# Modulation by matmuls, q and k by tokens, filter norms ahead of the taps, and a priority for the first run, in a hybrid diffusion step on one core

## The chip, the cores and the metric

The kernel runs on one core of a Trainium2 chip. The metric is the device time of one execution in microseconds (us). A core has five engines that run side by side, each with its own list of instructions: TensorE (PE in the profile, its weight loads as PEld), VectorE (DVE), ScalarE (ACT), GpSimd (POOL) and SyncE (SP), which here only issues DMAs. An instruction waits at the head of its engine's list until what it needs is there, and all that stands behind it on that engine waits too.

## The reference

One layer of a hybrid diffusion model, in fp32, on 2048 latent tokens (a grid of 32 by 64) and 256 prompt tokens, width 1024:

```python
shift1, scale1, gate1, shift2, scale2, gate2 = split(silu(cond) @ w_mod + b_mod, 6)
h = rms_norm(x, norm1_g) * (1 + scale1) + shift1
u_pool, u_hy, u_q, u_k, u_v = split(h @ w_in)          # 256, 3*256, 512, 512, 512 columns
y_pool = pool_mixer(u_pool)                            # window means, per-group linear
# Hyena: k = (mlp(z) @ f3_w) * decay, k / (sum over positions of |k| + 1e-6),
# two long convolutions by FFT, gated by a short convolution of u_hy
y_hy = hyena_mixer(u_hy, ...)
q = rms_norm(u_q per head of 64, q_norm_g); k = rms_norm(u_k per head of 64, k_norm_g)
y_na = attend(q, k, v)                                 # latent: 8x16 neighbourhood + 256 cached keys
x = x + gate1 * (concat(y_pool, y_hy, y_na) @ w_out)
h = rms_norm(x, norm2_g) * (1 + scale2) + shift2
x = x + gate2 * (square(relu(h @ w_up)) @ w_down)
```

The latent tokens and the prompt tokens have different conditioning vectors, so the modulation has two sets of six vectors of 1024. Outputs: both token sets, and the prompt's normalised k and its v.

## The kernel before

**Products.** Every wide product is made of three: each operand is split into a high and a low half (`split`, ACT or POOL makes the high half, DVE the low one as the difference), and `mm3` multiplies high by high, low by high and high by low. An accumulator in PSUM is 128 x 512. Weights come in tiles of 512 KB (`wtile`): a DMA, a high half (1024 columns a partition), a low half `wl` on DVE.

**Three streams.** The program is written as three generators that are woven by declared costs: `dense`, `latent_mixers` and `prompt_mixers`, the last two with priorities behind it (1000 and 2500). A scheduler then puts the instructions of each engine in an order by priority and readiness; that order is fixed when the program is built.

**dense.** `modulation_first` multiplies silu of both conditions by the first 2048 columns of w_mod: 16 slabs `wm` of 128 x 1024, four column strips of the PE array, 32 products (L239), then four transposes; this gives shift1 and scale1. The u projection follows in five runs of 512, 512, 512, 256 (the prompt) and 512 tokens, in the order UORD; a run normalises its 8 blocks of x (`normed`) and multiplies eight weight tiles `w_u`, each 24 products of 512 columns. The q, k and v projection (`proj_qkv`, runs in the order QORD) takes ten jobs a run. For q and k, channels are the rows of the result: a tile of 128 channels (two heads) by all tokens of the run, 24 products; ACT copies it and squares it, POOL and DVE split the square, two products with `headsum` (L265) add up the squares of a head's 64 channels and spread the sum over its 64 rows, `rstd` makes the root in six wide steps on ACT and DVE (L144 and L145 are the DVE ones), and DVE applies root and gain. For v, tokens are the rows: 128 tokens by 256 channels, 24 products of 256 columns. Then come the prompt's output projection and MLP, and those of the latent bands.

**The other four modulation vectors** (`modulation_rest`) are made in steps that `dense` interleaves with the jobs (MODU steps behind each u tile of a run, MODQ behind every second step of q, k and v): for each of 8 chunks of 512 columns and each of 8 slabs of 128 rows, DVE adds the slab times one condition to an accumulator (L338), ACT scales it by the other (L339) and POOL adds that (L340); at the end of a chunk eight products with ones (L346, 2 columns) add up the 128 partitions.

**Filters** (`filters`, in latent_mixers, beside the u projection). A small MLP with sines makes h2 (64 features, two directions, 2304 positions). `filter_taps` multiplies it by f3 (16 tiles of 128 positions for each of two filters, L405), DVE multiplies by the decay (L411), ACT takes the absolute value and POOL adds it up (L414). When all taps of a filter are there, `filter_rinv` adds over positions by products with ones, and POOL divides each tile (L419). Then comes the first half of the FFT (`time_to_freq`; the low half of its input is `ksl`). The rest of the Hyena mixer (`hyena`: the first halves for z, 16 groups of `spectrum` a filter, the inverse) runs beside q, k and v, the prompt's mixers too, and the latent attention after it.

**The order in time**, from the first and the last product of each: the first u product stands at 66 us; u runs to about 430 us; q, k and v to 1049; the Hyena mixer to about 1200; the latent attention from 1224 to 2000, with output projections and MLPs beside it; MLPs of the bands fill the rest.

The lines that the prediction's steps touch follow.

Of the kernel before, what the change touches and what calls it, by code (L numbers as in the profile page):

```python
# [10 lines left out]
F32 = mybir.dt.float32  # L11
# [8 lines left out]
P = 128  # L20
# [7 lines left out]
DH = 64  # L28
# [27 lines left out]
def tile_hybrid_step(ctx: ExitStack, tc: tile.TileContext, a: dict):  # L56
# [33 lines left out]
    headsum = ctile([P, P], "headsum", F32R)  # L90
    for e in range(2):
        for f in range(2):
            nc.gpsimd.memset(headsum[64 * e:64 * e + 64, 64 * f:64 * f + 64].bitcast(F32), float(e == f))

# [40 lines left out]
    def rstd(pool, ss, n, shape):  # L135

        r = pool.tile(shape, F32, tag="rsr", name="r", bufs=1)
        v = xp.tile(shape, F32, tag="tmp", name="v")
        t = xp.tile(shape, F32, tag="tmp", name="t")
# [80 lines left out]

    def modulation_first(lp):
# [18 lines left out]
        pmt = acc_tile()  # L240
        mrow = xp.tile([P, 512], F32, tag="raw", name="mrow", bufs=3)
        nc.vector.tensor_copy(mrow, pm)
        for q in range(4):
            nc.tensor.transpose(pmt[:, q * P:(q + 1) * P], mrow[:, q * P:(q + 1) * P], ident)
        pmv = pmt.rearrange("p (q j r) -> p j q r", q=4, j=4)

        def halves(t):
            return t.rearrange("p (j q) -> p j q", j=2)

# [6 lines left out]
    JOBS = ((1, 0), (1, 1), (1, 2), (1, 3), (2, 0), (0, 0), (0, 1), (0, 2), (0, 3), (2, 1))  # L256

    def proj_qkv(qp, hT, T0, n):
# [3 lines left out]
        def finish(comp, j, raw, sq):  # L262
            pss = aux_tile()[:, :n]
            for i in range(2):
                nc.tensor.matmul(pss, headsum, sq[i], start=(i == 0), stop=(i == 1))  # L265
            r = rstd(qp, pss, DH, [P, n])
            nc.vector.scalar_tensor_tensor(out=raw, in0=raw, scalar=(qg8, pvs("kg"))[comp], in1=r, op0=ALU.mult, op1=ALU.mult)
            nc.sync.dma_start(out=(qT, kT)[comp][j][:, T0:T0 + n], in_=raw)
            if comp == 1 and T0 == NL:
                nc.sync.dma_start(out=a["new_kT"][j * P:(j + 1) * P, :], in_=raw)  # L270

        def rows(dst, r0, cs):
            return dst[r0:r0 + 2 * P, cs].rearrange("(e p) c -> p e c", p=P)

        for comp, part in JOBS:
            if comp == 2:
                W = [wtile("w_v", 2 * part + kk, 4, (None, nc.gpsimd)[kk]) for kk in range(2)]
                cs = slice(part * 256, (part + 1) * 256)
                for t in range(0, n, 2 * P):
                    pp = acc_tile()  # L280
                    for e in range(2):
                        ts = slice(t + e * P, t + (e + 1) * P)
                        for k in range(KD):
                            mm3(pp[:, e * 256:(e + 1) * 256], hT[k][0][:, ts], hT[k][1][:, ts], W[k // 4][0][:, k % 4, :], W[k // 4][1][:, k % 4, :], k == 0, k == KD - 1, skip_group_check=True)
                        yield 2600
                        while todo:
                            finish(*todo.pop(0))
                    v = qp.tile([P, 2, 256], F32, tag="q", name="v")
                    nc.scalar.activation(v.rearrange("p e c -> p (e c)"), pp, AF.Copy)
                    if T0 < NL:  # L290
                        nc.sync.dma_start(out=rows(vd, T0 + t, cs), in_=v)
                    else:
                        nc.sync.dma_start(out=rows(vpd, 0, cs), in_=v)
                        nc.sync.dma_start(out=rows(a["new_v"], 0, cs), in_=v)
                continue
# [4 lines left out]
            while todo:  # L300
                finish(*todo.pop(0))
# [1118 lines left out]
```

## Time and profile before

| | |
|---|---|
| median of 3 executions | 3247.18 us (3244.32 to 3251.28) |
| the profiled execution | 3239.31 us, of which the span of its instructions is 3237.4 us |
| mean granted clock of PE | 0.959 |
| PE busy | 3008.9 us (93% of the span) |
| DVE busy | 2104.9 us (65%) |
| ACT busy | 1507.1 us (47%) |
| POOL busy | 1179.4 us (36%) |

These are averages over stages that differ. The page's slices show POOL and DVE at 30 to 90% in the first 15 of 40 slices (some 1200 us) and at 20 to 60% later, and PE's clock at 0.8 or 0.9 of its full rate in most of the first 15 and above 0.9 in all later ones. A wait in the rows below is put down to the instruction that ended last before it, which is not always the one that would have been late alone.

### The profile page before, as it was taken

To read this page: it belongs to the slowest core of one execution; us is meant where nothing else is said; L and a number is where in the kernel's file an instruction comes from. 1 tells how busy PE (TensorE), PEld (TensorE's weight loads), DVE (VectorE), ACT (ScalarE), POOL (GpSimd) and SP (SyncE) were. 2 spreads that over 40 slices of the span, in tenths; PEclk is the share of its full clock that TensorE was granted. 3 is DMA by queue.
4 is the path that set the end of the run, shared out by engine and by line. 5 is a ranking of instruction groups with operands and counts; after the bars stand their busy time and mean duration, and the time that the engine had idled before them with its cause. 6 is when DMAs were issued, how large, how long until landed. Compare 5 with 4: busy or idle time off the path is not lost.

```text
span 3237.4 us, 44877 instructions
## 1 busy us (share of the span) xinstructions
PE 3008.9 (93%) x15997; PEld 2483.3 (77%) x15997; DVE 2104.9 (65%) x3090; ACT 1507.1 (47%) x2803; POOL 1179.4 (36%) x996
## 2 busy tenths in 40 slices
PE   4989888878898899999999999899999999999999
PEld 1777677766777898986887777688878888788887
DVE  8797967997857977787666555544463444644443
ACT  3556455554656656666555554322342223432222
POOL 3777745566424523445333332311131111311111
PEclk8999888888998999999999999999999999999999
DMA  6657476556855596553334324322324223232322
GB/s 220 190 161 250 140 231 218 188 189 195 274 173 190 163 313 196 180 186 107 123 114 126 111 94 154 115 96 98 124 85 150 98 93 122 91 118 97 98 98 85
DMA packets 252862, 489.99 MB, mean 151 GB/s; under 512 B 23508, under 2 KB 124569, under 8 KB 252316
## 3 DMA queue, kind: packets, MB, share of 16 engines
q1 hardware_dynamic: 245437, 464.83, 44.1%
q0 software_dynamic: 7200, 22.28, 2.4%
q8 instruction: 127, 2.08, 0.3%
q14 instruction: 98, 0.79, 0.1%
HBM read 417.67 MB, written 70.13 MB: 151 GB/s over the span
## 4 chain that ended last, share of the span: by engine, by line
PE 68%; DVE 15%; DMA 6%; issue 4%; POOL 4%; ACT 3%; SPq 1%; DVEq 0%; ACTq 0%; POOLq 0%
PE pm L131 19%; PE pm L132 19%; PE pm L133 19%; PE po L867 3%; PE ppt L846 2%; DVE wl L120 2%; PE ps L832 1%; PE ps L833 1%; DMA dc<-in_decay 1%; POOL kk L419 1%; DVE macc L338 1%; DMA wm<-in_w_mod 1%; DVE hl L171 1%; PE pf L131 1%; POOL ssq L155 1%
## 5 line engine op out<-in xcount | busy, mean ns | idle before, releaser
L131 PE MATMUL pm<-hh,wh 128*128 128x512 f32 (+1 forms) x2240 | 850.0, 382 | 37.8 <-ACT hh L117 17.6
L120 DVE TENSOR_TENSOR wl<-wraw,wh 128x1024 fp32r<-128x1024 f32 x460 | 608.0, 1323 | 424.7 <-ACT wh L117 403.6
L132 PE MATMUL pm<-hl,wh 128*128 128x512 f32 (+1 forms) x2240 | 847.6, 379 | 16.7 <-DVE hl L171 12.4
L133 PE MATMUL pm<-hh,wl 128*128 128x512 f32 (+1 forms) x2240 | 845.1, 378 | 6.7 <-DVE wl L120 6.7
L117 ACT ACTIVATE wh<-wraw 128x1024 fp32r<-128x1024 f32 x430 | 454.5, 1058 | 765.7 <-PE pm L132 673.5
L120 POOL TENSOR_TENSOR al<-r,ah 128x512 fp32r<-128x512 f32 (+1 forms) x160 | 200.8, 1256 | 975.2 <-ACT ah L117 975.0
L131 PEld LDWEIGHTS pm<-hh,wh 128*128 128x128 f32 x2240 | 435.0, 195 | 116.8 <-ACT hh L117 19.1
L132 PEld LDWEIGHTS pm<-hl,wh 128*128 128x128 f32 x2240 | 434.6, 194 | 95.8 <-DVE hl L171 14.8
L133 PEld LDWEIGHTS pm<-hh,wl 128*128 128x128 f32 x2240 | 433.8, 194 | 81.9 <-DVE wl L120 8.0
L133 PE MATMUL pm<-ah,wl 128*128 128x512 f32 (+1 forms) x1280 | 475.8, 372 | 0.1
L131 PE MATMUL pm<-ah,wh 128*128 128x512 f32 (+1 forms) x1280 | 471.9, 372 | 4.0 <-ACT ah L117 2.5
L132 PE MATMUL pm<-al,wh 128*128 128x512 f32 (+1 forms) x1280 | 474.1, 371 | 1.2 <-POOL al L120 1.2
L1094 DVE SCALAR_TENSOR_TENSOR x<-pm,gate,x 128x512 f32<-128x512 f32 (+1 forms) x320 | 221.1, 695 | 273.3 <-PE pm L133 272.5
L131 PEld LDWEIGHTS pm<-ah,wh 128*128 128x128 f32 x1280 | 240.4, 188 | 47.0 <-ACT ah L117 2.7
L132 PEld LDWEIGHTS pm<-al,wh 128*128 128x128 f32 x1280 | 241.4, 189 | 43.7 <-POOL al L120 1.4
L133 PEld LDWEIGHTS pm<-ah,wl 128*128 128x128 f32 x1280 | 241.4, 189 | 41.8 <-issue 0.8
L838 POOL TENSOR_SCALAR sS<-sS,rl 128x736 f32<-128x736 f32 (+5 forms) x128 | 117.7, 920 | 201.1 <-DVE rl L837 127.2
L969 POOL TENSOR_TENSOR Tt<-bias,mask 128x360 f32<-128x360 f32 (+5 forms) x96 | 102.4, 1067 | 180.1 <-DVE m L981 147.5
L117 ACT ACTIVATE ah<-r 128x512 fp32r<-128x512 f32 (+1 forms) x160 | 93.8, 588 | 151.4 <-DVE r L1077 150.9
L155 POOL TENSOR_TENSOR ssq<-ssq,sqr 128x512 f32<-128x512 f32 (+1 forms) x70 | 97.7, 1396 | 135.5 <-ACT sqr L154 135.5
L986 ACT ACTIVATE sS<-sS,m 128x480 f32<-128x480 f32 (+5 forms) x128 | 77.2, 603 | 112.0 <-DVE m L985 107.7
L1077 DVE TENSOR_TENSOR r<-r 128x512 f32<-128x512 f32 (+1 forms) x160 | 118.1, 739 | 1.5 <-ACT r L1076 1.3
(317 smaller groups left out, 5044.7 us busy)
## 6 DMA issues: line engine op xcount, KB each, us to landing
wraw<-in_w_up SPq DMA_DIRECT2D x160, 512.0 KB
wraw<-in_w_down SPq DMA_DIRECT2D x160, 512.0 KB
wraw<-in_w_u SPq DMA_DIRECT2D x40, 512.0 KB
dftw<-in_S POOLq DMA_DIRECT2D x40, 512.0 KB, 6.4
wraw<-in_w_qk SPq DMA_DIRECT2D x40, 512.0 KB
wraw<-in_w_out SPq DMA_DIRECT2D x40, 512.0 KB
x<-in_xT_sample SPq DMA_DIRECT2D x64, 256.0 KB
wm<-in_w_mod SPq DMA_DIRECT2D x64, 256.0 KB
```

What stands on the lines that cost most here:

```text
L117: nc.scalar.activation(hi, raw, AF.Copy)
L120: lo_eng.tensor_tensor(out=lo, in0=raw, in1=hi.bitcast(F32), op=ALU.subtract)
L131: nc.tensor.matmul(out, lh, rh, start=start, stop=False, **kw)
L132: nc.tensor.matmul(out, lh, rl, start=False, stop=False, **kw)
L133: nc.tensor.matmul(out, ll, rh, start=False, stop=stop, **kw)
L155: nc.gpsimd.tensor_tensor(out=acc, in0=acc, in1=sq, op=ALU.add)
L838: nc.gpsimd.tensor_scalar(out=sc_[:, :tot], in0=sc_[:, :tot], scalar1=r, scalar2=1.0, op0=ALU.mult, op1=ALU.mult)
L867: nc.tensor.matmul(po[64 * e:64 * e + 64, ocol:ocol + P], vap(e, n), pt[:n, col * P:(col + 1) * P], start=(q == 0), stop=(q == len(chunks) ...
L969: nc.gpsimd.tensor_tensor(out=t_, in0=bias[e][:, bro:bro + nr, bco:bco + ncol], in1=mask[rc * 3 + cc_], op=ALU.add)
L986: nc.scalar.activation(sS[:, :n], sS[:, :n], AF.Exp, bias=m4[:, 2:3], accum_out=m4[:, 3:4])
L1077: nc.vector.tensor_tensor(out=r, in0=r, in1=r, op=ALU.mult)
L1094: nc.vector.scalar_tensor_tensor(out=xs[j], in0=po, scalar=gate2[:, j, c:c + 1], in1=xs[j], op0=ALU.mult, op1=ALU.add)
```

## The change

Four parts, in one diff.

1. *First run at the highest priority.* Loads of x, `modulation_first`, the statistics and the normalisations of the first run are written under a priority of 5000.
2. *Filter norms first.* Before any tap, 32 products of 512 fp32 columns compute every tap once with channels as rows; DVE multiplies by the transposed decay `dt`, ACT takes the absolute value and adds it up along the positions in the same instruction. The reciprocals go into `f3n`, so `normed_taps` yields taps that are divided already. POOL's accumulations and divisions, and `filter_rinv`, are gone.
3. *Modulation by matmuls.* `modulation_rest` takes two halves of 2048 columns; for each of 8 slabs of rows four products with `sc` (32 columns of weights, one column strip of PE each) go into one bank, and ACT or DVE adds the bank to a sum in SBUF; four transposes at the end of a half. Its 16 steps stand behind every second tile (MODU, MODQ).
4. *q and k by tokens.* They are computed as v is: 128 tokens are the rows, 256 channels (four heads) the columns, six jobs a run. The sum of squares of a head is a sum along a row on DVE, the root is made on 16 columns at most, DVE multiplies by it, four transposes turn the 256 tokens back to channels as rows, and ACT applies the gain on the way out. `headsum` is gone.

```diff
-    def rstd(pool, ss, n, shape):
+    def rstd(pool, ss, n, shape, size=None):
...
+    def modulation_rows(pmt, rows):
+        mrow = xp.tile([P, 512], F32, tag="raw", name="mrow", bufs=3)
+        nc.vector.tensor_copy(mrow, rows)
+        for q in range(4):
+            nc.tensor.transpose(pmt[:, q * P:(q + 1) * P], mrow[:, q * P:(q + 1) * P], ident)
...
-    JOBS = ((1, 0), (1, 1), (1, 2), (1, 3), (2, 0), (0, 0), (0, 1), (0, 2), (0, 3), (2, 1))
+    JOBS = ((1, 0), (1, 1), (2, 0), (0, 0), (0, 1), (2, 1))
...
+        def finish(comp, part, t, raw, r, out):
+            heads = raw.rearrange("p (e h d) -> p (e h) d", e=2, h=4)
+            nc.vector.tensor_tensor(out=heads, in0=heads, in1=r[:, t // 32:t // 32 + 8, None].to_broadcast([P, 8, DH]), op=ALU.mult)
+            tr = aux_tile()
+            for c in range(2):
+                for e in range(2):
+                    nc.tensor.transpose(tr[:, (2 * c + e) * P:(2 * c + e + 1) * P], raw[:, e * 256 + c * P:e * 256 + (c + 1) * P], ident)
+            nc.scalar.activation(out[:, :, t:t + 256], tr.rearrange("p (c t) -> p c t", c=2), AF.Copy, scale=(qg8, pvs("kg"))[comp])
...
+            for t in range(0, n, 2 * P):
+                pp = acc_tile()
+                for e in range(2):
+                    ts = slice(t + e * P, t + (e + 1) * P)
+                    for k in range(KD):
+                        mm3(pp[:, e * 256:(e + 1) * 256], hT[k][0][:, ts], hT[k][1][:, ts], W[k // 4][0][:, k % 4, :], W[k // 4][1][:, k % 4, :], k == 0, k == KD - 1, skip_group_check=True)
+                    if e == 0 and todo:
+                        finish(*todo.pop(0))
+                    yield 2600
+                v = qp.tile([P, 512], F32, tag="q", name="v", bufs=3)
+                nc.scalar.activation(v, pp, AF.Copy)
+                if comp < 2:
+                    sq = xp.tile([P, 512], F32, tag="tmp", name="sq")
+                    nc.scalar.activation(sq, v, AF.Square)
+                    nc.vector.tensor_reduce(out=ss[:, t // 32:t // 32 + 8], in_=sq.rearrange("p (h d) -> p h d", d=DH), axis=AX.X, op=ALU.add)
...
+            if comp < 2:
+                r = rstd(qp, ss, DH, [P, n // 32], "small")
...
+        for half in range(2):
+            acc = lp.tile([P, 512], F32, tag="macc", name="macc", bufs=1)
             for k in range(KD):
+                for g in range(4):
+                    wm.append(lp.tile([P, 512], F32, tag="wm2", name="wm2", bufs=4))
...
+                for g in range(4):
+                    nc.tensor.matmul(pb[32 * g:32 * g + 32, :], sc[:, k, :], wm[g], start=True, stop=True, skip_group_check=True)
                 if k == 0:
+                    nc.scalar.activation(acc, pb, AF.Copy)
                 else:
+                    nc.vector.tensor_tensor(out=acc, in0=pb, in1=acc, op=ALU.add)
...
+            with scope("norms") as fp:
+                sums = fp.tile([P, 8, 4], F32, tag="sums", name="sums", bufs=1)
...
+                                pf = psum()
+                                nc.tensor.matmul(pf, f3[r, o * 256 + c * P:o * 256 + (c + 1) * P], h2[r, b * 512:(b + 1) * 512], start=True, stop=True)
+                                junk = fp.tile([P, 512], F32, tag="junk", name="junk")
+                                nc.vector.tensor_tensor(out=junk, in0=pf, in1=dt, op=ALU.mult)
+                                nc.scalar.activation(junk, junk, AF.Abs, accum_out=sums[:, j, b:b + 1])
+                        yield 1700
...
+                nc.vector.tensor_tensor(out=f3n, in0=pf, in1=f3, op=ALU.mult)
...
-                    ri = filter_rinv(fp, psum, acc)
                     if o:
                         yield from wait_for("u", "ln")
...
-                        filter_finish(fp, o, kf, 0, ri, i == 0)
-                        filter_finish(fp, o, kb, 1, ri, i == 0)
...
-    MODU, MODQ = (0, 1, 1, 1, 2), (0, 2, 2, 1, 1)
+    MODU, MODQ = (0, 1, 1, 1, 0), (0, 1, 1, 1, 1)
...
+                with tc.high_priority(FIRST):
+                    xs = norm1_load(lp, 0, 512)
+                    modulation_first(m1)
+                    r = norm1_stats(lp, xs)
...
-                    for _ in range(MODU[i]):
+                    for _ in range(MODU[i] if step % 2 else 0):
                         next(mods, None)
```

The line numbers shift: mm3 is L131 to L133 before and L126 to L128 after.

**SP at the start.** SP issues the loads. `x` are blocks of the input, `wm` of 1024 columns the slabs of `modulation_first`, `wm` of 512 columns those of `modulation_rest`, `wraw` weight tiles, `z` the position features of the filter network, `pv` the small vectors (conditions, biases, gains). Before:

```order
L443 DMA z<-in_zT 33x2x2304
L385 DMA f_744<-in_f_w 64x512 x2
L73 DMA pv<-in_pv 128x112
L75 DMA kv<-in_kv 128x34
L315 DMA x<-in_xT_sample 128x512 x8
L236 DMA wm<-in_w_mod 128x1024 x8
L315 DMA x<-in_xT_sample 128x512
L127 DMA wraw<-in_w_u 128x1024 x3
L333 DMA wm_1131<-in_w_mod 128x512
L333 DMA wm_1247<-in_w_mod 128x512
L236 DMA wm<-in_w_mod 128x1024 x8
```

After, behind 8 blocks of x, 8 slabs, the small filter weights and z:

```order
L73 DMA pv<-in_pv 128x112
L75 DMA kv<-in_kv 128x34
L322 DMA x<-in_xT_sample 128x512
L122 DMA wraw<-in_w_u 128x1024 x3
L343 DMA wm_1175<-in_w_mod 128x512
L343 DMA wm_1177<-in_w_mod 128x512
L343 DMA wm_1179<-in_w_mod 128x512
L343 DMA wm_1181<-in_w_mod 128x512
L1192 DMA rsd<-r 1x512
L244 DMA wm<-in_w_mod 128x1024 x2
L122 DMA wraw<-in_w_u 128x1024
L244 DMA wm<-in_w_mod 128x1024 x6
```

x and the first 8 slabs moved ahead of z and pv; the last slabs got one more weight tile, two more slabs of the rest and the store of r in front of them.

**PE in the u projection.** `pm` is the accumulator of a u tile, `hh` and `hl` the halves of the input, `n` the auxiliary bank, `macc` the sum of `modulation_rest`. Before:

```order
L133 MATMUL pm<-hh,wl 128x512 x2
L131 MATMUL pm<-hh,wh 128x512
L346 MATMUL n<-ones,macc 128x2 x4
L131 MATMUL pf<-ksh,dftw 128x256
L346 MATMUL n<-ones,macc 128x2
L132 MATMUL pf<-ksl,dftw 128x256
L133 MATMUL pf<-ksh,dftw 128x256
```

After, at the first group of modulation products (the last row is a product of the norms):

```order
L126 MATMUL pm<-hh,wh 128x512
L346 MATMUL n<-wm_1527,sc 32x512
L346 MATMUL n<-wm_1529,sc 32x512
L346 MATMUL n<-wm_1531,sc 32x512
L346 MATMUL n<-wm_1533,sc 32x512
L127 MATMUL pm<-hl,wh 128x512
L128 MATMUL pm<-hh,wl 128x512
L126 MATMUL pm<-hh,wh 128x512
L127 MATMUL pm<-hl,wh 128x512
L511 MATMUL pf<-h_394,f_739 128x512
```

Eight sums over macc at the end of a chunk gave way to four products on four slabs, once a step, and each norm product stands alone among u products.

**PE at the end of q, k and v.** `pf` is a bank of the spectrum, whose operands are `skh`/`skl` (the filter), `s2h`/`s2l` (the signal) and `ysh`/`ysl` (their product). Before, the last sum over heads stands here, and the next dense product (the prompt's output projection) two rows later:

```order
L265 MATMUL n<-sqh,headsum 128x512
L131 MATMUL pf<-s2h,S2d 128x256
L132 MATMUL pf<-s2l,S2d 128x256
L133 MATMUL pf<-s2h,S2d 128x256
L131 MATMUL pf<-s2h,S2d 128x256
L132 MATMUL pf<-s2l,S2d 128x256
L133 MATMUL pf<-s2h,S2d 128x256
L265 MATMUL n<-sql,headsum 128x512
L131 MATMUL pf<-ysh,S2d 128x256
L131 MATMUL pm<-hh,wh 128x256
L132 MATMUL pm<-hl,wh 128x256
L133 MATMUL pm<-hh,wl 128x256
```

After, the first rows are the last products of v, and `pb` from `sS` belongs to the prompt's attention:

```order
L127 MATMUL pm<-hl,wh 128x256
L128 MATMUL pm<-hh,wl 128x256
L126 MATMUL pf<-ysh,S2d 128x256
L127 MATMUL pf<-ysl,S2d 128x256
L128 MATMUL pf<-ysh,S2d 128x256
L126 MATMUL pf<-ysh,S2d 128x256
L127 MATMUL pf<-ysl,S2d 128x256
L128 MATMUL pf<-ysh,S2d 128x256
L953 MATMUL pb<-ident,sS 128x128 x4
L126 MATMUL pf<-skh,S2d 128x256
L127 MATMUL pf<-skl,S2d 128x256
L128 MATMUL pf<-skh,S2d 128x256
```

From there to the next dense product stand 289 products, 223 of them of the spectrum, the others of the prompt's attention; the longest such run in the order of before has 56.

## Rows read from the trace of the kernel before

**Rows 1.** Stretches: us, busy (instructions) of PE, PEld, DVE, ACT, POOL; clock, DMA, GB/s.

```profile
66.00:430.00 364.00, 311.69 (x1411) 251.00 (x1412) 306.46 (x364) 184.56 (x298) 260.73 (x180) 0.89 0.58 182
430.00:1230.00 800.00, 690.64 (x4255) 610.45 (x4254) 641.38 (x834) 462.84 (x856) 387.28 (x354) 0.91 0.67 216
1230.00:2000.00 770.00, 761.85 (x4950) 622.32 (x4950) 530.21 (x1189) 447.81 (x1123) 296.93 (x287) 0.99 0.42 130
2000.00:3237.40 1237.40, 1214.58 (x5278) 993.51 (x5278) 575.05 (x616) 387.70 (x493) 215.13 (x154) 0.99 0.33 109
```

**Rows 2.** Waits of PE, 66 to 430 us: total us, times, longest.

```profile
PE pf L132 <- DVE ksl L120: 10.8, 7, 2.6
...
PE n L543 <- DVE S2m L350: 0.4, 1, 0.4
```

**Rows 3.** Waits of PE, 430 to 1230 us.

```profile
PE n L265 <- DVE sql L120: 12.3, 12, 1.9
PE pf L131 <- ACT F L590: 11.6, 7, 3.8
...
PE pm L131 <- DVE x L1057: 0.6, 1, 0.6
```

**Rows 4.** Groups of DVE by shape, whole run: busy us, mean ns | idle before.

```profile
L338 DVE SCALAR_TENSOR_TENSOR macc<-wm,sc,macc 128x512 f32<-128x512 f32 x56 | 54.6, 976 | 16.9 <-DMA wm<-in_w_mod 16.8
L984 DVE TENSOR_REDUCE m<-ps 128x1 f32<-128x256 f32 x128 | 53.5, 418 | 60.8 <-PE ps L833 60.3
...
L144 DVE SCALAR_TENSOR_TENSOR t<-t,v 128x512 f32<-128x512 f32 x40 | 36.4, 910 | 31.9 <-ACT t L143 31.9
...
L145 DVE SCALAR_TENSOR_TENSOR r<-t,r 128x512 f32<-128x512 f32 x40 | 33.7, 842 | 0.8
L120 DVE TENSOR_TENSOR sql<-sq,sqh 128x512 fp32r<-128x512 f32 x32 | 30.3, 946 | 15.7 <-POOL sqh L119 15.7
...
L411 DVE TENSOR_TENSOR kk<-pf,dc 128x512 f32<-128x512 f32 x32 | 21.6, 682 | 12.2 <-DMA dc<-in_decay 11.5 <-PE pf L405 0.6
```

**Rows 5.** The low half of a weight tile, 66 to 430 us, then 2000 us on.

```profile
L120 DVE TENSOR_TENSOR wl<-wraw,wh 128x1024 fp32r<-128x1024 f32 x40 | 66.5, 1662 | 8.9 <-ACT wh L117 8.9
...
L120 DVE TENSOR_TENSOR wl<-wraw,wh 128x1024 fp32r<-128x1024 f32 x217 | 270.0, 1245 | 341.2 <-ACT wh L117 335.7
```

**Rows 6.** Groups of POOL, 66 to 430 us.

```profile
L419 POOL TENSOR_TENSOR kk<-kk,rinv 128x512 f32<-128x512 f32 x32 | 52.8, 1686 | 1.1 <-DVE rinv L395 1.1
L414 POOL TENSOR_TENSOR acc<-acc,ab 128x512 f32<-128x512 f32 x32 | 49.4, 1552 | 25.5 <-ACT ab L413 25.2
L340 POOL TENSOR_TENSOR macc<-macc,wm 128x512 f32<-128x512 f32 x30 | 45.8, 1528 | 43.3 <-ACT wm L339 43.0
```

**Rows 7.** Groups of PE, whole run; then PE's timeline: start, us, records.

```profile
L346 PE MATMUL n<-ones,macc 128*128 128x2 f32 x128 | 17.4, 254 | 3.9 <-DVE macc L338 3.6 <-POOL macc L340 0.3
...
L159 PE MATMUL n<-ssq,ones 128*128 128x512 f32 x8 | 4.4, 631 | 0.3 <-POOL ssq L155 0.3
...
51.19 1.92 PE L239 MATMUL pm<-wm,sc 128*32 128x512 f32 x16
...
374.47 1.09 PE L543 MATMUL n<-ident,cy 128*128 128x128 f32 x4 [5.45 <-DVE halo L532]
```

**Rows 8.** Stretches that PE fills: with products of 256, then of 512 columns.

```profile
1150.00:1200.00 50.00, 50.00 (x429) 50.00 (x429) 37.15 (x49) 32.65 (x51) 11.24 (x17) 1.00 0.92 312
2150.00:2200.00 50.00, 50.00 (x221) 41.12 (x220) 21.54 (x24) 15.83 (x20) 6.44 (x5) 1.00 0.29 95
```

**Rows 9.** PE's timeline at the first u products [idle before and its releaser].

```profile
66.40 1.65 PE L131 MATMUL pm<-hh,wh 128*128 128x512 f32 x3 [5.24 <-ACT hh L117]
...
79.21 0.80 PE L132 MATMUL pm<-hl,wh 128*128 128x512 f32 x1 [7.53 <-DVE hl L171]
```

**Rows 10.** PE's timeline where the spectrum is nearly alone.

```profile
1040.92 0.58 PE L131 MATMUL pf<-ysh,S2d 128*128 128x256 f32 x1 [3.82 <-ACT F L590]
...
1050.98 0.58 PE L131 MATMUL pf<-ysh,S2d 128*128 128x256 f32 x1 [1.54 <-ACT ysh L117]
```

More of the change, by code (lines that the diff above doesn't have):

```diff
@@ L89, in tile_hybrid_step @@
     nc.vector.memset(epsc, EPS)
[L90 to L93, printed above, removed]
     uT = [dtile([P, T], f"uT{i}") for i in range(8)]
@@ L239, in modulation_first @@
                     nc.tensor.matmul(pm[r:r + 32, :], sc[:, k, :], wm[:, j * 512:(j + 1) * 512], start=(k == 0), stop=(k == KD - 1), skip_group_check=True)
[L240 to L248, printed above, removed]
+        pmv, halves = modulation_rows(acc_tile(), pm)
         for c in range(2):
@@ new lines, in finish @@
+        def finish(comp, part, t, raw, r, out):
[6 more added lines that the diff above has]
+            nc.scalar.activation(out[:, :, t:t + 256], tr.rearrange("p (c t) -> p c t", c=2), AF.Copy, scale=(qg8, pvs("kg"))[comp])
+            if t + 256 < n:
+                return
+            for c in range(2):
+                j = 2 * part + c
+                nc.sync.dma_start(out=(qT, kT)[comp][j][:, T0:T0 + n], in_=out[:, c])
+                if comp == 1 and T0 == NL:
+                    nc.sync.dma_start(out=a["new_kT"][j * P:(j + 1) * P, :], in_=out[:, c])
@@ L341, in modulation_rest @@
                 yield 600
-            pb = aux_tile()
-            for c in range(2):
-                for j in range(4):
-                    q = 2 * (c * 4 + j)
-                    nc.tensor.matmul(pb[:, q:q + 2], acc[c][:, j * P:(j + 1) * P], ones[:, 0:2], start=(q == 0), stop=True, skip_group_check=True)
-            pbv = pb[:, 0:16].rearrange("p (c j e) -> p c j e", c=2, e=2)
-            dst, nm = ((gate1, "bm_g1"), (S2m, "bm_s2"), (G2, "bm_c2"), (gate2, "bm_g2"))[kind]
-            for c in range(2):
-                nc.vector.tensor_tensor(out=dst[:, half * 4:half * 4 + 4, c], in0=pbv[:, c, :, 0], in1=pvs(nm, half * 4, 4), op=ALU.add)
+            pmv, halves = modulation_rows(aux_tile(), acc)
@@ L351, in modulation_rest @@
+            for j, (dst, nm) in enumerate((((gate1, "bm_g1"), (S2m, "bm_s2")), ((G2, "bm_c2"), (gate2, "bm_g2")))[half]):
+                for c in range(2):
+                    nc.vector.tensor_tensor(out=halves(dst[:, :, c]), in0=pmv[:, 2 * j:2 * j + 2, :, c], in1=halves(pvs(nm, 0, 8)), op=ALU.add)
             yield 1000
```

145 lines of the change are left out of this document (75 added, 70 removed).

## The prediction

> **What bounds the kernel now.** I read the table by stretches first [rows 1]. From 1230 us to the end TensorE is busy 761.9 of 770.0 and 1214.6 of 1237.4 us at a granted clock of 0.99: nothing that a vector engine saves can shorten that, and the change touches no line there. What lies before is different. Until the first product of the u projection at 66.4 us [rows 9] the kernel waits for the modulation vector. From 66 to 1230 us TensorE is busy 311.7 of 364.0 and 690.6 of 800.0 us, at 0.89 and 0.91 of the clock. That is 52.3 + 109.4 = 161.7 us of idle time; and as the clock has two levels (1.2 and 2.4 GHz), 0.89 and 0.91 mean that it stood at the lower one for 22% and 18% of these stretches, after such gaps, which costs up to 40 + 72 = 112 us more. So of 1164 us TensorE needs some 890 at full rate (77%). DVE is busy 306.5 and 641.4 us there, 948 of 1164 (81%), as much as TensorE's own need. The waits say which of the two sets the pace: in the first stretch the rows of TensorE's waits that name DVE run from ksl to S2m, 9 rows that sum to 45.0 of 52.3 us [rows 2]; in the second 11 rows, from sql to x, 40.2 of 109.4 us [rows 3]. DVE therefore ends 85 of 162 us, about half; the rest ends on ACT for the most part. This is a stretch that two engines share, not one with a single bound.
>
> **The start.** x, the first 8 slabs of w_mod and the statistics move ahead of the filter network on SP, TensorE, ACT and DVE; z and pv go behind them. It is less than it looks: in both orders all 16 slabs, three weight tiles and x must land before the modulation is whole, and the order of after puts one more weight tile, two more slabs of the rest and the store of r ahead of the last six. The same bytes at the same rate give no earlier last slab. What can go is what stood after it: the first product came at 66.40 us, and the second weight product only at 79.21 after a wait on hl, which stood on DVE behind filter work [rows 9]; in the new order hl follows the normalisations almost directly. I take 7 us off, with 0 and 14 (most of 79.21 − 66.40) as ends.
>
> **What DVE loses between 66 and 1230 us.** Removed: 56 modulation steps, 54.6 us, and 8 first steps at the same price, 7.8 [rows 4]. For q and k, 32 wide rounds of four instructions (two of the root, the low half of the square, the gain): 32 × (910 + 842 + 946 + 842 ns) = 113 us, where the gain is priced as the second root step; 8 rounds of half the width, 14 us. Together 190 us. Added: 36 sums over head columns; the nearest row is a reduction of 256 columns at 418 ns, so 418 to 836 for 512; 627 gives 23 us. 36 products with the root, at 842: 30. 32 products of the norms and 14 additions from PSUM, at 682: 31 [rows 4]. 40 root steps on 16 columns, below 418 each, 10 us at 250. Together 94. Net 96 us less; with the reduction at either end 88 to 104.
>
> DVE also gets faster where POOL is quiet. The low half of a weight tile takes 1662 ns between 66 and 430 us, with POOL busy 260.7 of 364.0 us (72%), and 1245 after 2000 us [rows 5], with POOL busy 215.1 of 1237.4 us (17%) [rows 1]. POOL loses the accumulations of the modulation and of the norms and the scaling of the taps, 45.8 + 49.4 + 52.8 = 148 of its 260.7 us there [rows 6], which leaves 31%. On the line between the two prices that gives about 1350 ns; 40 tiles × 0.3 = 12 us, and I add half as much for other instructions of DVE that read what lies in SBUF: 18 us, from 12 to 25. DVE's relief is 114 us.
>
> **What TensorE gains in work.** q and k: 768 products of 512 columns and 192 of 256 become 1728 of 256. The stretch that is dense in 512s holds 221 in 50 us (226 ns), the one of 256s 429 in 50 us (117 ns) [rows 8]: 202.2 − 173.6 − 22.5 = +6 us. Norms: 32 products of 512 fp32 columns; the nearest is the column sum of the statistics, 4.4 us for 4 whose last parts overlap other work (8 records, two for an fp32 product) [rows 7]: 0.97 each is taken, 31 us, and 35 at most. Modulation: 16 groups of four products in four column strips, 1.92 us for two such groups (16 records) [rows 7]: 15, against 17.4 us of the old column sums that go [rows 7]. 36 groups of four transposes, 1.09 us by the row, of which the last part overlaps the next product, so from 0.6: 22 to 39, and 25 is taken, nearer to the low end since in a dense order it always overlaps. Against them 80 head sums, 64 × 226 + 16 × 117 ns = 16 us. Small rest (mrow, rib, less the sums of the taps): −1. That is +43 us, with 40 and 61 as ends. Taps and decays of the second filter move behind u; their count stays the same. ACT's saved instructions are not counted: they are slack where DVE or TensorE is late.
>
> **Waits.** Three new ones stand in TensorE's own order. The sums of q and k no longer wait for squares: those waits, 12.3 us on sql, go [rows 3]. The transposes that come instead stand 48 to 126 u, q, k or v products behind the last product of their tile (36 groups), over 5.6 us at 117 ns; the chain before them (copy, square, sum, six root steps, product) has no row of its own on ACT; at DVE's 842 for a wide step and 250 for a small one it costs 2 × 842 + 627 + 6 × 250 + 842 ns = 4.7 us, so it is hidden while neither engine is far behind; with the cover gone it is up to 36 × 4.7 = 167 us, which would be a run slower than before by itself. Modulation products wait for slabs, four at a time with four buffers; one group per two u steps (24 products × 226 ns × 2 = 10.8 us) hides a transfer. The norms go through two PSUM banks, one product per some ten others: a DVE product of 682 ns is hidden by 2 us of others.
>
> **The sum.** If DVE kept its share of 81%, 114 us of relief would shorten the stretch by 140 us; TensorE would then need 890 + 43 = 933 of 1024 us, 91%, against 77% now, with chains from engine to engine still in between. If DVE's relief bought nothing, the stretch would lengthen by TensorE's 43. As DVE ends about half of TensorE's waits [rows 2, 3], I take half of 140, 70 us: 1094 us, with TensorE needing 85% and DVE at 76%. With the start: 3239.3 − 70 − 7 = 3162 for a profiled execution (span 3237.4 and 1.9 around it), and the median of three is 7.9 above that one: **3170 us**; its own range is 3130 to 3215.
>
> **A rule that speaks against it.** In this trace narrow products cost little more: 2 × 117 against 226 ns [rows 8], so halving the columns is worth 6 us. The Trainium skill, TensorE: Matmul & The Clock Gate, section Back-to-back issue gap, says that weight load and product together set the spacing, about 81 ns at 128 columns and 131 at 512. By an estimate on the line between these figures 256 columns would take 98 ns, and the 768 wide products would cost 49 us more instead of 6, which makes 3213. The trace disagrees at 512 columns (226 ns).
>
> **Rivals.**
> - *TensorE sets the pace (slower).* Its waits are the tails of chains that stay as long as before; DVE's relief only lengthens DVE's idle time, and 43 us of fp32 norms, modulation and transposes are added between 66 and 1230 us: 3239.3 − 7 + 43 + 7.9 = 3283. For it: TensorE is already busy 86% there [rows 1], and over half of the second stretch's waits do not name DVE [rows 3]. Against: sql goes, and 45 of 52 us in the first stretch are DVE's [rows 2]. It decides once waits and low clock together shrink by less than 36 us.
> - *A hole behind q, k, v.* In the new order the prompt's convolution and attention slide behind the first spectrum; 289 products then stand in a row without a dense one, 223 of them of the second spectrum. At 117 ns they take 34 us; but the spectrum, 36 products a group, starts a group 10.1 us after the last one where little else is dense [rows 10], and 6.2 groups take 63 us. That is 29 us more: 3199. Against: DVE, busy 641.4 of 800 us [rows 1], has less to do.
> - *The priority does nothing at the start*, since pv and the last slabs come as late: 3177.
> - *Narrow products wait for their weights.* A load takes 41.12 / 221 = 186 ns [rows 8]; if it were not hidden, the pairs would cost 768 × (372 − 226) = 112 us; half of that in place of the 6 gives 3170 + 56 − 6 = 3220. Against: in the row of 256s loads and products are both busy all 50 us at 117 ns. The rule above is the same rival at its own price.
> - *Full relief*: DVE keeps its share, 3239.3 − 7 − 140 + 7.9 = 3100.
> - *No change*: relief and extra work cancel, 3247.
>
> **How the numbers follow.** Forecast 0.48, hole 0.14, priority idle 0.08, full relief 0.08, narrow products 0.04, no change 0.05, slower 0.13. Faster by over 0.2% (about what a measurement of this kernel tells from no change) is 0.82, within it 0.05, slower 0.13. The range leaves out most of the slower case and the lowest part of full relief: 3105 to 3262.
>
> **What would show it.** First u product and second weight product: before 66 and 79 us, expected 3 to 10 earlier. TensorE idle from there to the start of attention: under 110 us against 161.7, clock above 0.93. DVE some 95 to 115 us less busy there, POOL at least 56 × 1.53 + 49.4 + 52.8 = 188 us less over the run [rows 6], wl below 1450 ns in the u projection. Narrow products 117 to 120 ns apart. It is wrong if TensorE's idle time stays, if waits on norms or modulation slabs appear over 15 us each, or if behind q, k, v TensorE is busy under 60% for over 60 us.

## The result and the profile after

The changed kernel takes **3208.5 us** (median of 4, 3195.9 to 3209.6) against 3249.2 for the kernel before: a ratio of 0.987, 95% interval 0.984 to 0.990. The prediction said 3170, from 3105 to 3262. The direction holds; of 77 us forecast, 41 came. One execution with one convolution buffer (5076 us) and one with the priority alone (5469 us) ran at a much lower clock and are left out of the times below; with the first, that kernel's median is the 3188.5 us which the expectations name, without it 3186.8.

(One correction to what stands ahead: the numbers 1000 and 2500 of the two latter streams lift their instructions ahead of `dense`; they are not behind it.)

The profiled execution after took 3209.6 us, span 3207.8. These are its stretches, cut where stages end: first u product, end of u, end of q, k and v, last product of the prompt's attention, first and last product of the latent attention (columns as in [rows 1]).

```profile
0.00:58.40 58.40, 24.48 (x102) 5.64 (x102) 30.42 (x65) 20.02 (x27) 15.48 (x17) 0.97 0.79 273
58.40:390.00 331.60, 314.36 (x1445) 220.82 (x1445) 243.74 (x372) 173.97 (x305) 109.63 (x86) 0.96 0.67 214
390.00:940.00 550.00, 507.65 (x3725) 473.77 (x3726) 372.70 (x522) 268.76 (x531) 218.99 (x207) 0.96 0.69 225
940.00:1030.00 90.00, 67.17 (x350) 53.75 (x349) 68.92 (x110) 51.92 (x113) 39.54 (x31) 0.80 0.41 128
1030.00:1133.00 103.00, 84.55 (x640) 81.98 (x640) 67.76 (x92) 54.26 (x93) 34.90 (x43) 0.91 0.82 258
1133.00:1872.00 739.00, 719.71 (x4948) 599.80 (x4948) 525.62 (x1199) 443.88 (x1121) 297.21 (x287) 0.99 0.45 138
1872.00:3207.80 1335.80, 1313.19 (x5697) 1070.47 (x5696) 613.39 (x661) 417.04 (x537) 228.71 (x163) 0.99 0.33 107
```

The same three stages of the kernel before (start; q, k and v; from there to the latent attention):

```profile
0.00:66.40 66.40, 30.18 (x110) 6.01 (x111) 52.19 (x91) 24.54 (x35) 19.30 (x23) 0.85 0.69 246
...
430.00:1049.00 619.00, 527.72 (x3011) 453.83 (x3009) 491.36 (x626) 354.71 (x676) 320.30 (x287) 0.91 0.65 208
1049.00:1224.60 175.60, 158.56 (x1217) 153.10 (x1217) 144.84 (x197) 104.95 (x174) 64.69 (x66) 0.93 0.73 238
```

The latent attention starts at 1133 instead of 1224.6 us, 92 earlier, yet the end comes only 30 earlier (span 3207.8 against 3237.4). The lead is partly an illusion of order: before, 924 products of 256 columns of the output projections and MLPs stood ahead of the attention, after 534, so 390 × 117 ns = 46 us of the same work was merely put off. The new feature is the fourth row: 90 us behind q, k and v in which TensorE is busy 67 us at a clock of 0.80. There is the hole of the second rival, and its waits (us in total, times, longest) are links of the spectrum's chain:

```profile
PE pf L126 <- DVE Yt L650: 7.8, 5, 2.2
PE pf L126 <- ACT sg L661: 6.0, 7, 1.6
PE pf L126 <- ACT ysh L112: 3.8, 4, 1.6
```

To compare whole executions I use a **ledger** of TensorE. Idle time is the span less PE's busy time on the page. The time of each PE record (up to the start of the next) times the granted clock in it, summed, is the work at full clock; what is left is lost to the low clock. Profiled executions, us:

| kernel | span | idle | lost to low clock | work at full clock |
|---|---|---|---|---|
| before | 3237.4 | 228.5 | 93.7 | 2915.2 |
| changed | 3207.8 | 176.7 | 64.3 | 2966.8 |
| changed, one convolution buffer | 3188.4 | 159.2 | 63.3 | 2966.0 |
| changed, no norms | 3142.5 | 152.7 | 54.4 | 2935.4 |
| changed, no norms, one convolution buffer | 3162.2 | 170.3 | 57.7 | 2934.2 |
| modulation and q, k, one convolution buffer | 3172.4 | 175.6 | 56.6 | 2940.2 |
| modulation by matmuls alone | 3227.0 | 214.4 | 79.8 | 2932.8 |
| q and k by tokens alone | 3220.3 | 209.7 | 88.8 | 2921.8 |
| priority alone | 3280.2 | 261.4 | 97.4 | 2921.4 |

So the change took 52 us of idle time and 29 us of low clock away and added 52 us of work: 30 us in these executions. The medians differ by 41; the profiled execution of before is 8 to 10 us faster than the medians. The last column is not a count of products alone: between before and priority alone, which have the same products, it differs by 6 us, so a few us in it are order.

The prices after, first of PE, then of DVE (busy us, mean ns | idle before), the answers to [rows 7], [rows 4] and [rows 5]; the last row is of 58 to 390 us:

```profile
L511 PE MATMUL pf<-h,f 64*128 64x512 f32 x64 | 36.8, 659 | 3.9 <-DVE junk L514 3.1 <-DVE fx L484 0.8
...
L346 PE MATMUL n<-wm,sc 128*32 128x512 f32 x128 | 24.3, 605 | 0.5 <-DMA wm<-in_w_mod 0.5
L271 PE MATMUL n<-ident,v 128*128 128x128 f32 x144 | 22.1, 277 | 1.8 <-DVE v L267 1.6
```

```profile
L267 DVE TENSOR_TENSOR v<-v,r 128x512 f32<-128x512 f32 x36 | 26.6, 774 | 0.6
L303 DVE TENSOR_REDUCE ss<-sq 128x8 f32<-128x512 f32 x36 | 24.4, 679 | 24.1 <-ACT sq L302 24.0
L514 DVE TENSOR_TENSOR junk<-pf,dt 128x512 f32<-128x512 f32 x32 | 21.8, 684 | 21.0 <-PE pf L511 9.9 <-DMA dt<-in_decayT 7.9 <-ACT macc L348 2.4
```

```profile
L115 DVE TENSOR_TENSOR wl<-wraw,wh 128x1024 fp32r<-128x1024 f32 x40 | 53.1, 1329 | 25.1 <-ACT wh L112 23.5 <-PE n L594 1.3 <-PE pm L128 0.2
```

### The profile page after: what moved, and what is told of

The parts are those of the page before. It is cut to its first block, busy times and chain, and to the rows that moved or that the text cites. A ratio compares the mean times of both kernels' runs of the same rounds, so it can differ in the third digit from the quotient of the medians.

```text
span 3207.8 us, 46233 instructions
## 1 busy us (share of the span) xinstructions
PE 3031.1 (94%) x16901; PEld 2506.2 (78%) x16901; DVE 1922.6 (60%) x3017; ACT 1429.8 (45%) x2722; POOL 944.5 (29%) x832
## 4 chain that ended last, share of the span: by engine, by line
PE 65%; DVE 2%; DMA 1%; ACT 1%; issue 1%; POOL 1%; SPq 0%; ACTq 0%; POOLq 0%; DVEq 0%
PE pm L126 18%; PE pm L128 18%; PE pm L127 18%; PE po L918 3%; PE ppt L897 3%; PE ps L883 1%; PE ps L884 1%; DMA yraw<-yT 1%; PE pf L126 0%; PE pf L127 0%; PE pf L128 0%; POOL ssq L150 0%; PE pbo L957 0%; DVE xn L169 0%; DVE wl L115 0%
## 5 line engine op out<-in xcount | busy, mean ns | idle before, releaser
L126 PE MATMUL pm<-hh,wh 128*128 128x512 f32 (+1 forms) x1920 | 721.0, 378 | 29.0 <-ACT hh L112 14.7
L127 PE MATMUL pm<-hl,wh 128*128 128x512 f32 (+1 forms) x1920 | 718.8, 375 | 1.6 <-POOL hl L115 1.6
L128 PE MATMUL pm<-hh,wl 128*128 128x512 f32 (+1 forms) x1920 | 719.5, 375 | 0.0
L126 PE MATMUL pm<-ah,wh 128*128 128x512 f32 (+1 forms) x1280 | 473.6, 372 | 4.9 <-ACT r L1127 4.0
L128 PE MATMUL pm<-ah,wl 128*128 128x512 f32 (+1 forms) x1280 | 476.4, 373 | 0.0
L126 PEld LDWEIGHTS pm<-hh,wh 128*128 128x128 f32 x1920 | 366.6, 191 | 104.2 <-ACT hh L112 17.2
L128 PEld LDWEIGHTS pm<-hh,wl 128*128 128x128 f32 x1920 | 366.2, 191 | 76.8 <-issue 15.5
L127 PEld LDWEIGHTS pm<-hl,wh 128*128 128x128 f32 x1920 | 366.8, 191 | 75.0 <-issue 9.4
L126 PEld LDWEIGHTS pm<-ah,wh 128*128 128x128 f32 x1280 | 241.1, 189 | 48.2 <-ACT r L1127 4.2
L128 PEld LDWEIGHTS pm<-ah,wl 128*128 128x128 f32 x1280 | 241.7, 189 | 42.6 <-issue 1.5
L126 PE MATMUL pm<-wh,hh 128*128 128x256 f32 x864 | 248.5, 292 | 4.4 <-ACT hh L112 3.9
L127 PE MATMUL pm<-wl,hh 128*128 128x256 f32 x864 | 248.1, 290 | 4.5 <-DVE wl L115 4.4
L128 PE MATMUL pm<-wh,hl 128*128 128x256 f32 x864 | 248.9, 292 | 3.1 <-POOL hl L115 3.1
L126 PEld LDWEIGHTS pm<-wh,hh 128*128 128x128 f32 x864 | 166.8, 194 | 11.1 <-ACT hh L112 5.8
L127 PEld LDWEIGHTS pm<-wl,hh 128*128 128x128 f32 x864 | 167.5, 194 | 7.6 <-DVE wl L115 5.5
```

The costliest lines, as they stand in the source:

```text
L126: nc.tensor.matmul(out, lh, rh, start=start, stop=False, **kw)
L127: nc.tensor.matmul(out, lh, rl, start=False, stop=False, **kw)
L128: nc.tensor.matmul(out, ll, rh, start=False, stop=stop, **kw)
```

## The experiments

All on the chip, each against runs of the kernel before on the same chip (3246.7 to 3250.3). Four things were in question: whether the hole behind q, k and v holds the missing gain, what each part is worth with the others, what it is worth alone, and whether the priority does anything. The runs were taken on three chips, on which the kernel before took 3250.3, 3246.7 and 3249.0 us, so a difference between runs of two chips is good to some 4 us.

### The hole: one buffer less

In the built program the prompt Hyena's pool starts at byte 159,200 of a partition, since the pools of the rest of the modulation and of q, k and v grew by 2048 and 4352 bytes; the pool of the latent mixer's first spectrum ends at 161,120. They overlap by 1920 bytes, and the prompt's mixers stand still after their filters (last product at 490 us) until that spectrum is over: its last product starts at 767 us, their next load is issued at 770. Before, the pools lay 4 KB apart, and that load was issued at 649 us, over 100 us ahead of the spectrum's last product. Two ways of taking 2 KB away:

```diff
-        u = hy.tile([P, L], F32, tag="cu", name="cu", bufs=2)
+        u = hy.tile([P, L], F32, tag="cu", name="cu", bufs=1)
...
-        y = hy.tile([P, L], F32, tag="cy", name="cy", bufs=2)
+        y = hy.tile([P, L], F32, tag="cy", name="cy", bufs=1)
```

> The changed kernel, with one buffer instead of two for the two tiles of the prompt's short convolution (cu, cy). That makes the prompt Hyena's pool 2 KB smaller, so it no longer lies on memory that the latent mixer's first spectrum uses (161,248 against an end of 161,120; in the changed kernel 159,200). Theory 1, the hole is a memory overlap and costs time: the prompt's attention ends before q, k and v do, the stretch of 90 us behind q, k and v in which TensorE was busy 67 us at a clock of 0.80 goes, and with it 23 us of idle time and some 14 us of low clock: 3172 us, from 3160 to 3185. Theory 2, the latent chain sets the end and the dense work only moves: idle time turns up elsewhere and the time stays within 6 us of 3208.5.

Measured: **3186.8 us** (3182.5 to 3190.2), ratio 0.981 (0.979 to 0.982).

```diff
-                v = qp.tile([P, 512], F32, tag="q", name="v", bufs=3)
+                v = qp.tile([P, 512], F32, tag="q", name="v", bufs=2)
```

> The changed kernel with two instead of three buffers for the copies of q, k and v: the same 2 KB, taken from another pool. Theory 1 (memory overlap): the same gain as with one convolution buffer, within 8 us, though waits of ACT on a free copy may cost some of it: 3165 to 3190 us. If the gain of the other run came from the convolution's buffers themselves, this run stays at 3208. Theory 2 (the end is set by the latent chain): both stay at 3208.

Measured: **3198.5 us**, 0.984 (0.983 to 0.986). In both the hole is gone: with one convolution buffer that load is issued at 519 us, and the prompt's attention ends at 817 and 821 us. The same 70 us in the changed kernel, then with one convolution buffer:

```profile
960.00:1030.00 70.00, 52.27 (x253) 41.05 (x253) 50.98 (x82) 38.11 (x83) 30.37 (x24) 0.77 0.32 98
```

```profile
960.00:1030.00 70.00, 57.17 (x397) 54.60 (x396) 61.76 (x85) 41.59 (x76) 35.64 (x29) 0.85 0.64 204
```

144 more instructions went through TensorE, the longest stretch without a dense product ahead of the latent attention fell from 92.6 to 32.3 us, but the gain is 22 and 10 us instead of 37: both times lie between the ranges of the two theories. The stretch is no full one now either: a chain from spectrum to inverse remains in it. And filling has a price elsewhere: with one convolution buffer, idle time and low clock behind q, k and v fall from 63 to 37 us, but during q, k and v, where the prompt's attention now stands, they rise from 59 to 69.

### Without the norms, with and without the overlap

Part 2 undone: taps, absolute values on ACT, sums and divisions on POOL as before.

```diff
-            with scope("norms") as fp:
...
-                        kf, kb = normed_taps(fp, psum, f3n, o, lambda r, e: h2[r, i + e:NL:16], lambda d: a["decay"][d, :, i:i + 2, :])
...
+                    ri = filter_rinv(fp, psum, acc)
...
+                        filter_finish(fp, o, kf, 0, ri, i == 0)
+                        filter_finish(fp, o, kb, 1, ri, i == 0)
```

With one convolution buffer:

> The changed kernel with one convolution buffer (no overlap), and with the filters as before: taps first, POOL adds up and divides. Compared with 3188.5 us. By the prediction's sum the norms cost TensorE 31 us and DVE 22 us and relieve POOL of 102 us, which makes DVE some 12 us faster: without them the kernel is 15 to 37 us faster, 3150 to 3173. The rival: POOL's chain sets the pace of the u projection (adding up, dividing, then the FFT), and without the norms the kernel is slower, 3200 to 3225.

Measured: **3163.5 us**, 0.974 (0.973 to 0.976): 23 us faster than with the norms. And with two buffers, so with the overlap:

> The changed kernel with the filters as before, and with the overlap of pools (159,200 against 161,120). Without the overlap it took 3163.5 us. In the order of this kernel the last product of the prompt's attention stands ahead of the last one of q and k, so dense work does not run out: if the overlap costs only through that hole, 3163 within 6; if it costs by itself, 3183 (the 20 us of the changed kernel) or more.

Measured: **3144.6 us**, 0.968 (0.966 to 0.970), the fastest of all, 64 us ahead of the changed kernel (2%). Neither expectation holds: here the overlap does not cost 22 us, it gives 19. (It does hold the prompt back: the load that was issued at 770 us in the changed kernel is issued at 703 us with it and at 601 without.) From the end of q, k and v to the latent attention, first with the overlap, then without:

```profile
962.00:1098.30 136.30, 121.86 (x958) 118.93 (x958) 108.42 (x146) 81.28 (x136) 49.93 (x55) 0.94 0.79 261
```

```profile
972.00:1119.00 147.00, 127.91 (x985) 124.45 (x984) 115.20 (x155) 86.30 (x147) 52.47 (x58) 0.91 0.76 248
```

With the overlap the prompt's attention ends at 957 us, 5 us before q, k and v do (962), so dense work never runs out; without it, at 858. Idle time over the run is 152.7 against 170.3 us. A late prompt is thus no harm in itself: it puts its small products beside more of q, k and v. It harms where it ends after them, as in the changed kernel (1030 against 940 us). This reading fits both pairs; it was not tried by moving the prompt alone.

### Without the priority, and the priority alone

```diff
-                with tc.high_priority(FIRST):
-                    xs = norm1_load(lp, 0, 512)
-                    modulation_first(m1)
-                    r = norm1_stats(lp, xs)
+                xs = norm1_load(lp, 0, 512)
+                modulation_first(m1)
+                r = norm1_stats(lp, xs)
...
```

> The changed kernel without the priority of the first run. By the prediction's step on the start the first u product comes some 7 us later than with it (58.4 us) and the time is 3216 us (3209 to 3223). The rival that the priority does nothing: 3208. A third reading, that early filter work matters more than an early first run, would make it faster than 3205.

Measured: **3196.5 us** (3194.0 to 3206.1), 0.983 (0.982 to 0.985). With one convolution buffer:

> The changed kernel without the priority of the first run and with one convolution buffer (no overlap). If the priority is worth the 7 us of the prediction: 3195. If what it gains at the start is given back within the u projection: 3188 within 5. If the 12 us by which the kernel without the priority was faster than the changed kernel are real: 3176.

Measured: **3196.3 us**, 0.985 (0.983 to 0.986). Without the overlap the priority is worth some 10 us (3186.8 against 3196.3), near the 7 forecast. With the overlap the changed kernel is not faster for it: 3208.5 against 3196.5, which is the number of the third reading, but the two intervals overlap. And by the medians the buffer bought nothing here (the two profiled executions differ by 10 us), though the stretch without a dense product fell from 76.9 to 16.4 us: the third sign that a hole's length is not its price.

> The kernel before with the priority of the first run alone. By the prediction's step on the start, 7 us faster than before, 3243 against 3250 (3236 to 3250). If the gain at the start is given back, since the same filter work is still to be done: 3250 within 4.

Measured: **3281.4 us**, 1.010 (1.008 to 1.012): 35 us *slower* than before. Neither expectation held. The first u product comes at 58.0 us, as hoped, but the first taps come 37 us later (first row of before, second of the priority alone):

```profile
90.77 1.26 PE L405 MATMUL pf<-f,h 64*128 64x256 f32 x8
```

```profile
128.01 1.26 PE L405 MATMUL pf<-f,h 64*128 64x256 f32 x8
```

Its waits of TensorE up to 430 us are led by

```profile
PE n L159 <- POOL ssq L155: 23.5, 2, 19.5
PE n L543 <- DVE halo L532: 14.0, 2, 7.6
PE pf L131 <- ACT ksh L117: 13.3, 4, 6.2
```

The first of these is no loss: 19.5 of its 23.5 us are TensorE's first wait of all, for the statistics that the priority put in first place, and the changed kernel has the same wait (18.9 us). The u projection ends at 437 us instead of 422; idle time is 17 us more there (68.6 against 51.9) and 18 us more between the end of q, k and v and the latent attention (34.8 against 17.0). What delays the first taps is seen in the 72 us from the first u product on, against the same part of the kernel before (second row; columns as in [rows 1]):

```profile
58.00:130.00 72.00, 54.98 (x205) 40.83 (x206) 67.38 (x92) 37.05 (x53) 34.30 (x23) 0.83 0.43 132
66.00:130.00 64.00, 53.45 (x201) 39.73 (x202) 52.89 (x60) 34.09 (x52) 49.13 (x33) 0.85 0.51 165
```

DVE is busy 67.4 of 72 us (94%), with the normalisations, the filter network and the short convolution in turn; before it was 52.9 of 64. POOL is busy less than before. So what is moved ahead pushes the filter network back on DVE. That this delay makes the 35 us was not tried by itself, and a delay alone is not enough: in the pair with modulation and q, k changed (below) the first taps also come 20 us later with the priority (101.9 against 81.7 us), and that kernel is faster for it.

### The parts with and without each other

Modulation as before, the rest changed (part 3 undone):

```diff
-                    nc.tensor.matmul(pb[32 * g:32 * g + 32, :], sc[:, k, :], wm[g], start=True, stop=True, skip_group_check=True)
...
+                    nc.vector.scalar_tensor_tensor(out=acc[0], in0=wm, scalar=sc[:, k, 0:1], in1=acc[0], op0=ALU.mult, op1=ALU.add)
+                    nc.scalar.activation(wm, wm, AF.Copy, scale=sc[:, k, 1:2])
+                    nc.gpsimd.tensor_tensor(out=acc[1], in0=acc[1], in1=wm, op=ALU.add)
```

> The changed kernel with the other four modulation vectors made as in the kernel before (by DVE, ACT and POOL). Its pools do not overlap (161,248 against 161,120), so it is compared with the changed kernel with one convolution buffer, 3188.5 us. By the prediction's sum the modulation by matmuls takes 53 us net off DVE and is even for TensorE; half of that at 1.23 us each is 33 us: 3222 (3208 to 3235). If only the engine that is late at the moment counts and that is not DVE: 3188.

Measured: **3223.4 us**, 0.993 (0.991 to 0.994): 37 us for the modulation by matmuls, 33 expected.

q and k as before, the rest changed (part 4 undone):

```diff
-    JOBS = ((1, 0), (1, 1), (2, 0), (0, 0), (0, 1), (2, 1))
+    JOBS = ((1, 0), (1, 1), (1, 2), (1, 3), (2, 0), (0, 0), (0, 1), (0, 2), (0, 3), (2, 1))
...
+                nc.tensor.matmul(pss, headsum, sq[i], start=(i == 0), stop=(i == 1))
+            r = rstd(qp, pss, DH, [P, n])
```

> The changed kernel with q and k computed by channels as in the kernel before (head sums by products, wide root steps), all else changed. Its pools do not overlap (163,552 against 161,504), so there is no hole by theory 1. By the sum of the prediction q and k by tokens relieve DVE of 64 us and cost TensorE some 15 us of the 43; half of that relief at 1.23 us of time each is 39 us. So without it the time is 3172 + 39 = 3211 us where theory 1 holds, 3195 to 3225; if q and k by tokens are worth nothing by themselves it is near 3172, and if theory 2 holds (no cost of the hole) near 3240.

Measured: **3217.6 us**, 0.990 (0.988 to 0.991): 31 us for q and k by tokens, against the run without overlap.

Each of the two alone on the kernel before, and both together:

> The kernel before with modulation by matmuls alone. By the prediction's sum (53 us off DVE, half of it at 1.23 us each, nothing for TensorE) 33 us faster than before, and by the run that left it out 35: 3212 to 3216. If DVE's relief only pays once POOL's filter chain is shortened too: 3235 to 3247.

Measured: **3229.2 us**, 0.993 (0.992 to 0.995): 20 us, between the two expectations.

> The kernel before with q and k by tokens alone. By the prediction's sum 39 us faster less some 15 us of TensorE work, by the run that left it out 29: 3208 to 3223. If it only pays with the other parts: 3240 or more.

Measured: **3225.2 us**, 0.992 (0.991 to 0.994): 24 us, just outside the first range.

> The kernel before with modulation by matmuls and q and k by tokens, and with one convolution buffer (no overlap); no norms ahead of the taps and no priority. The same with the priority took 3163.5 us. If the priority is worth the 8 us that it was worth with the norms (3196.3 against 3188.5): 3171. If the priority costs where the filters are as before, since it holds back the filter network and POOL's chain behind it (it cost 35 us alone): 3130 to 3158.

Measured: **3177.0 us**, 0.978 (0.976 to 0.979): 72 us, where the two alone sum to 44. In the ledger too: alone they cut idle time by 14 and 19 us, together by 53. A reading that fits: one engine less in a chain is worth more when the next one has been relieved as well. No run isolates it, and the run of both also has one convolution buffer, which was not tried without it. With these two in place the priority gains: 3177.0 without it, 3163.5 with it, 13.5 us, outside both expectations and the opposite of the 35 us that it costs alone.

## Why the prediction was right, and where it was not

**The start: right.** First u product 58.45 us against 66.40 [rows 9], second weight product 60.70 against 79.21:

```profile
58.45 1.29 PE L126 MATMUL pm<-hh,wh 128*128 128x512 f32 x3 [4.51 <-ACT hh L112]
60.70 0.79 PE L127 MATMUL pm<-hl,wh 128*128 128x512 f32 x1 [0.96 <-POOL hl L115]
```

Without the priority the changed kernel has that product at 68.7 us, so the priority makes the lead. What the prediction did not see is that such a start can be paid for: alone it cost 35 us.

**DVE's relief: more than forecast.** DVE's busy time fell by 182 us over the run (2104.9 to 1922.6), where 114 was forecast. Of this some 120 us are instructions that went less those that came, where 96 was counted, and some 60 those that stayed and got faster, where 18 was. The prices were near: the reduction took 679 ns (627 taken), the products 774 (842), the norms' products 684 (682); the gain that went took some 1000 ns, not 842. Not counted were the reciprocals and sums of the filters that halved (L394 and L395, 16 to 8 us). POOL fell from 1179.4 to 944.5 us, and the low half of a weight tile in the u projection from 1662 [rows 5] to 1329 ns (1350 forecast); beyond it many others got faster, such as those of two columns in the short convolution (776 to 311 ns). The Trainium skill, SBUF — State Buffer, section Who interferes with whom, says that DVE's second pair of ports is shared with GpSimd; the wl rows agree, 1662 ns with POOL busy 72% and 1329 with 33%.

**TensorE's work: +52 instead of +43.** From the ledger by kind: norms +31 (31 forecast), the modulation +8 (−2 forecast: a group of four products came to 1.4 us, not to the 0.96 of the row that was read), transposes 13 less 21 for the head sums (+9 forecast, −8 came), and the dense products +23 in all. Of these, narrow products in q, k and v took 127 ns at full clock and the wide ones of q and k 235, so 1728 × 127 − 768 × 235 − 192 × 124 ns = +15 us, not 6; the u products took 244 ns instead of 239, and the products of v some 3 ns more. The estimate from the Trainium skill, TensorE: Matmul & The Clock Gate, section Back-to-back issue gap, was 49 us: no run here shows its 131 ns at 512 columns, and the measurement decides.

**The sum: the step that failed.** I set two ends, −140 if DVE kept its share and +43 if its relief bought nothing, and then took half of 140. But half way between these ends is −48, not −70; the work that I had just priced was left out. With −48 the forecast would have been 3192. That this is near the 3186.8 us without the hole is in part luck: the same rule fed with what was measured, 182 us of relief at 1.23 each and 52 us of work, gives half of −224 + 52, or −86, and 3154. What was mis-sized is the worth of DVE's relief: the forecast asked 113 us of idle time and low clock to go between 66 and 1230 us and 7 at the start for 114 us of relief; 81 went over the run, for 182. Part of the rest is the hole: it was a rival with 29 us, and it came about, longer than that rival said (93 us without a dense product, where it had 63) and from a cause that the prediction does not name, the overlap of pools; filling it gave 22, 10 and, without the priority, nothing. The late stages gave back some more: from the latent attention on, 14 us of idle time and low clock that were not there before. Of the prediction's signs, idle time from the first u product to the attention came to 101 us (under 110 said) at a clock of 0.94, and none of its signs of being wrong appeared: behind q, k and v TensorE was busy 75%, above its mark of 60%, and still the hole cost time.

**The parts by their prices: right one by one.** By the prediction's prices the modulation is worth 33 us (37 measured), q and k by tokens 39 less 15 of TensorE's work, 24 (31; the expectation above forgot the 15), the priority 7 (10), and the norms cost 15 to 37 (23), all with the other parts in place and without the overlap. Alone on the kernel before, the first three are worth 20, 24 and −35; the norms alone were not tried. That the norms cost could have been read ahead of time from the same text: 31 us of fp32 products and 22 us of DVE against relief on POOL, an engine that ended few of TensorE's waits.

**The rivals.** "TensorE sets the pace" was half true: DVE's 182 us bought 81. "Narrow products wait" is out: a pair of them took 254 ns, where that rival had 372. "No change", "full relief" and a priority that does nothing at the start are out.

## What to carry to other kernels

Price a change part by part and ask of each part whether it pays: with the others in place all four came out near their prices here, three of them gains and the fourth a loss of 23 us, with the overlap of 64. Relief of one engine and added work on another are summed with their signs before anything is halved, and a part's value is not a constant: two parts were worth 44 us alone and 72 together, and the priority −35 alone and +10 to +14 beside other parts, without the overlap. When pools grow, compare their addresses with their neighbours': an overlap of 1920 bytes moved the end of the prompt's mixers from 817 to 1030 us, past the dense work in one version, and into a good place in another.

## What was unexpected

A stretch of 93 us without a dense product was worth 22 us when filled, one of 77 us nothing: the chain that made it was still there, and filling it cost waits in the stage ahead. And the start: 8 us won at the first product turned into 35 us lost at the end. The longest wait in that run's list, 19.5 us on POOL, has no part in it: it lies before the first u product, and the changed kernel has it too.
